# Token-major one-hot tiles for the gate matrices of two PEER stages, all made by VectorE

## The chip, the cores and the metric

One core of a Trainium2 chip runs the whole program. The metric is the device time of one execution in microseconds (us); less is better.

## The reference, cut to what matters

The program is two transformer layers over 512 tokens of width 1024. Each ends in a PEER feed-forward step, which picks 16 of 16384 experts for each of 8 heads and each token:

```python
def peer_ffn(h, w_query, sub_keys, expert_u, expert_v):
    def chunk(xc):                                   # 128 tokens
        q = (xc @ w_query).reshape(128, 8, 2, 128)
        s1 = einsum('thc,hnc->thn', q[:, :, 0], sub_keys[:, 0])
        s2 = einsum('thc,hnc->thn', q[:, :, 1], sub_keys[:, 1])
        ...                                          # top 16 of each, then top 16 of the sums
        eidx = e1 * 128 + e2                         # (t, 8, 16): 128 experts a token
        gate = softmax(top)
        act = gelu(einsum('td,thkd->thk', xc, expert_u[eidx]))
        return einsum('thk,thkd->td', gate * act, expert_v[eidx])
```

## The kernel before, in words

The kernel does a PEER step in three stages.

*Route.* The expert indices (`E`, `ei`) and the gates (`GT`) are found for all 512 tokens; VectorE does the top-16 searches.

*Gate matrices* (lines 1160 to 1213), for the first 384 tokens (`ND = 3` tiles of 128; the fourth tile is done by gathered rows, in the main loop). A token has 128 slots (8 heads by 16), and its gates are wanted as a dense matrix of 128 by 128 over all 16384 experts. An expert's number has 14 bits: 3 high ones, 4 middle ones and 7 low ones. They are transposed so that the slots lie on the partitions and the tokens along the free dimension (`sT[0]`, `sT[1]`, `sT[2]` in bf16; `sT[3]` holds the gates in fp32). For each group of `TG = 32` tokens three small tiles are made: `oa_` (one-hot of the 3 high bits, then times the gate) and `ob_` (one-hot of the 4 middle bits). For each 8 tokens two large ones follow: `oh2` (one-hot of the low 7 bits, 128 columns a token) and `oh1` (the product of `oa_` and `ob_`, again 128 columns a token). One fp32 matmul a token, `oh2` transposed times `oh1`, is the token's matrix. The profile records an fp32 matmul as two instructions, so that 384 tokens make 768 records a stage. Four tokens share a PSUM tile (`pgg`, two buffers); ScalarE copies it into a staging tile `stg`, and two DMAs a group write that to DRAM (`Gd`), 12 groups a stage. In the profile `oha`, `ohb` and `oh` are these tiles.

Both large tiles have the layout (128 columns, 8 tokens), tokens innermost: a token's operand in the matmul, `oh2[:, :, 4 * q + j]`, takes one fp32 element in every eight, 32 bytes apart. Of the `oh1` products VectorE makes one in four and GpSimd three.

*Main loop* (from line 1259): 128 steps over blocks of 128 experts. Step e takes the gates of its block from DRAM (`gbuf`, four blocks a load), multiplies them with the activations `ga` of that block (`w`, VectorE, line 1270), splits the product (`wh` on ScalarE, `wl` on VectorE) and multiplies it with the V rows into `y`. The activations come from a unit A for each block (`emit_A`): a DMA of the U block (`ur`), a rounded copy on ScalarE (`uh`, L1100), the remainder on GpSimd (`ul`, L1106), 24 matmuls into `pa` (L1113, L1114, L1116) and a Gelu on ScalarE. Units run `NA = 28` blocks ahead of the loop: 19 are issued during the routing, `TB = 3` ahead of the gate matrices, 4 among them (`RG`), 2 behind them, so 9 in and around the gate stage.

The routing has a fixed order. In the gate stage each engine's order is made by the scheduler of the framework from the program and its own estimate of costs; each engine then works through its list in order, and waits where an operand or a buffer isn't free.

Of the kernel before, what the change touches and what calls it, by code (L numbers as in the profile page):

```python
# [14 lines left out]
OP = mybir.AluOpType  # L15
# [8 lines left out]
def build(tc, I, out, dbg=None, stop=None):  # L24
# [22 lines left out]
    V, A, G, T, S = nc.vector, nc.scalar, nc.gpsimd, nc.tensor, nc.sync  # L47
# [706 lines left out]
    for h2 in range(2):  # L754
        if h2 == 1:
            ws = keep_w(wk, I["w_mem_o"], 8, 0)
        for t in range(NT):
# [3 lines left out]
            for hh in range(2):  # L761
# [10 lines left out]
                for j in range(2):  # L772
# [3 lines left out]
                            in1=zs.unsqueeze(2).broadcast_to([128, 2, 256]), op=OP.mult)  # L776
# [59 lines left out]
        o_ += 16 // (i + 1)  # L836
    NC = o_ + 8
    CE = G
    O1 = 3
    TA = 3  # L840
    GS = 2
    GE = 99
# [3 lines left out]
    EF = 120  # L846
    EV = 100
    EW = 120
    GM = 4
    GR = 3  # L850
    TB = 3
    NA = 28

    def queries(qp, Wq, hi, lo):
# [197 lines left out]
    TG = 32  # L1052
# [18 lines left out]
    def peer(keysT_d, U, UT, Vt, front, finish, nm, side=None, also=None, then=None):  # L1071
# [37 lines left out]
        def a_mm(e):  # L1109
# [46 lines left out]
        r1 = rp.enter_context(tc.tile_pool(name=nm + "r1", bufs=1))  # L1156
# [3 lines left out]
        iota = r1.tile([128, 128], F32, name="iota")  # L1160
# [8 lines left out]
        sT = [r1.tile([128, NDT], F32 if j == 3 else BF16, name=f"sT{j}") for j in range(4)]  # L1169
# [7 lines left out]
        ix.close()  # L1177
        run_ahead(TB)
        rw = rp.enter_context(tc.tile_pool(name=nm + "gg", bufs=2))
        irep = r1.tile([128, 128, 8], BF16, name="irep")  # L1180
        V.tensor_copy(out=irep, in_=iota.unsqueeze(2).broadcast_to([128, 128, 8]))
        irtg = r1.tile([128, 16, TG], BF16, name="irtg")
        V.tensor_copy(out=irtg, in_=iota[:, 0:16].unsqueeze(2).broadcast_to([128, 16, TG]))
        for tg in range(NTG):
            stg = rw.tile([128, 128, TG], F32, name="stg", tag="stg")

            def row(j, c0, n, m):
                return sT[j][:, c0:c0 + n].unsqueeze(1).broadcast_to([128, m, n])

            c0 = tg * TG  # L1190
            oa_ = rw.tile([128, 8, TG], F32, name="oha", tag="oha")
            V.tensor_tensor(out=oa_, in0=irtg[:, 0:8], in1=row(0, c0, TG, 8), op=OP.is_equal)
            V.tensor_tensor(out=oa_, in0=oa_, in1=row(3, c0, TG, 8), op=OP.mult)
            ob_ = rw.tile([128, 16, TG], F32, name="ohb", tag="ohb")
            V.tensor_tensor(out=ob_, in0=irtg, in1=row(1, c0, TG, 16), op=OP.is_equal)
            for t8 in range(TG // 8):
                tk = slice(t8 * 8, t8 * 8 + 8)
                oh2 = rw.tile([128, 128, 8], F32, name="oh2", tag="oh2")
                V.tensor_tensor(out=oh2, in0=irep, in1=row(2, c0 + t8 * 8, 8, 128), op=OP.is_equal)  # L1199
                oh1 = rw.tile([128, 128, 8], F32, name="oh1", tag="oh1", bufs=O1)  # L1200
                (V if (tg * 4 + t8) % GM == GR else G).tensor_tensor(
                    out=oh1.rearrange("p (a b) t -> p a b t", a=8), in0=oa_[:, :, tk].unsqueeze(2).broadcast_to([128, 8, 16, 8]),
                    in1=ob_[:, :, tk].unsqueeze(1).broadcast_to([128, 8, 16, 8]), op=OP.mult)
                for q in range(2):
                    pg = psm.tile([128, 4, 128], F32, name="pgg", tag="mm")
                    for j in range(4):
                        T.matmul(pg[:, j, :], oh2[:, :, 4 * q + j], oh1[:, :, 4 * q + j], start=True, stop=True)  # L1207
                    ts = t8 * 8 + 4 * q
                    A.copy(out=stg[:, :, ts:ts + 4].rearrange("p e t -> p t e"), in_=pg)
            S.dma_start(out=Gd[0][:, tg], in_=stg[:, 0:G0])  # L1210
            S.dma_start(out=Gd[1][:, tg], in_=stg[:, G0:])
            if tg in RG:
                run_ahead(1)
        vrs = {e: load_v(e) for e in range(2)}
        rp.close()
        pctx.close()
        run_ahead(NA)
        nev = 0
# [40 lines left out]
        for e in range(128):  # L1259
# [9 lines left out]
            with tc.manual_schedule(engines={mybir.EngineType.Pool, DVE_}):  # L1269
# [24 lines left out]
            for t in range(ND):  # L1294
                ts = slice(t * 128, (t + 1) * 128)
# [9 lines left out]
        row = then() if then else (lambda t, psum: None)  # L1305
# [102 lines left out]
    if stop == "h2":  # L1408
# [347 lines left out]
    def fin2(t, acc, pool, psum):  # L1756
# [116 lines left out]
```

## Time and profile before

| | us |
|---|---|
| median of 3 runs | 4033.55 |
| lowest, highest | 4032.31, 4042.46 |
| the profiled execution | 4039.25 |
| its span | 4037.5 |
| start of the first gate stage (first `oha`) to first `y` matmul | 743.04 to 970.62 |
| the same of the second | 2859.16 to 3086.76 |

TensorE is busy for 96% of the span, VectorE for 77%, GpSimd for 53%, ScalarE for 41%. The two gate stages are the stretches from about 743 to 970 us and from 2859 to 3087 us. A share over the span says little of them; they are read from windows, from the groups of instructions by line in that stretch, and from the timeline. In a timeline a row's first two numbers are its start and its length; instructions of one engine overlap a little, so the step from one start to the next is what an instruction costs in a dense row of them.

### The profile page before, as it was taken

How to read it: one execution, taken by the hardware profiler on the slowest of the kernel's cores; microseconds unless marked ns; L12 is line 12 of the kernel's file. 1: busy time of each engine (PE TensorE's matmuls, PEld its weight loads, DVE VectorE, ACT ScalarE, POOL GpSimd, SP SyncE). 2: the span in 40 equal slices, each digit the busy share in tenths (PEclk: the TensorE clock that was granted, in tenths of full speed). 3: DMA queues.
4: the chain of work that ended last, by engine and by line, in shares of the span. 5: the costliest groups of instructions: out<-in, count | busy, mean ns of one | idle time of the engine just before them, and what ended most of it. 6: DMA issues, size and time to landing. Idle time of an engine off the chain costs nothing. (4 is left out here: it accounts for less than half of the span.)

```text
span 4037.5 us, 53263 instructions
## 1 busy us (share of the span) xinstructions
PE 3859.8 (96%) x19062; PEld 3367.6 (83%) x19062; DVE 3101.3 (77%) x5460; ACT 1659.2 (41%) x2567; POOL 2146.8 (53%) x1333
## 2 busy tenths in 40 slices
PE   6999999899999999999899988999899999999999
PEld 5767788899899999987777766788899999999987
DVE  8456589884898888877756566689885898888875
ACT  3454432454333333333444567332454333333333
POOL 3000047654788887750424433257655778887750
PEclk8999999999999999999999989999999999999999
DMA  3333132235999889987222322332236999999884
GB/s 112 98 102 115 61 112 74 103 133 195 313 332 316 314 315 314 328 286 261 91 81 58 93 73 93 116 111 78 106 136 218 320 324 316 315 317 314 303 272 151
DMA packets 330057, 784.31 MB, mean 194 GB/s; under 512 B 32048, under 2 KB 148864, under 8 KB 326400
## 3 DMA queue, kind: packets, MB, share of 16 engines
q1 hardware_dynamic: 252608, 499.86, 37.6%
q0 software_dynamic: 77184, 281.05, 19.5%
q8 instruction: 150, 2.46, 0.2%
q14 instruction: 115, 0.94, 0.1%
HBM read 722.98 MB, written 56.65 MB: 193 GB/s over the span
## 5 line engine op out<-in xcount | busy, mean ns | idle before, releaser
L1106 POOL TENSOR_TENSOR ul<-ur,uh 128x1024 fp32r<-128x1024 f32 x256 | 713.7, 2788 | 263.9 <-ACT uh L1100 177.1
L1113 PE MATMUL pa<-phi,uh 128*128 128x384 f32 x2048 | 695.1, 339 | 0.6 <-ACT ga L1118 0.6
L1114 PE MATMUL pa<-plo,uh 128*128 128x384 f32 x2048 | 694.2, 339 | 0.0
L1300 PE MATMUL y<-vl,wh 128*128 128x512 f32 x1536 | 599.8, 392 | 5.7 <-DVE vl L1273 5.7
L1301 PE MATMUL y<-vh,wl 128*128 128x512 f32 x1536 | 601.8, 393 | 0.0
L1299 PE MATMUL y<-vh,wh 128*128 128x512 f32 x1536 | 595.6, 392 | 1.7 <-ACT vh L1272 1.6
L1273 DVE TENSOR_TENSOR vl<-vr,vh 128x1024 fp32r<-128x1024 f32 x256 | 341.4, 1334 | 216.1 <-ACT vh L1272 215.9
L1248 DVE SCALAR_TENSOR_TENSOR acc<-vrow,act,acc 128x1024 f32<-128x1024 f32 x256 | 423.6, 1655 | 50.0 <-DMA vrow<-in_expert_v_dram,ei 25.3
L1237 DVE SCALAR_TENSOR_TENSOR urow<-urow,hgat 128x1024 f32<-128x1024 f32 x256 | 416.5, 1634 | 28.9 <-DMA urow<-in_peer_u_dram,ei 17.4
L1271 ACT CAST wh<-w 128x384 fp32r<-128x384 f32 x256 | 131.4, 513 | 745.8 <-PE y L1300 607.0
L1116 PE MATMUL pa<-phi,ul 128*128 128x384 f32 x2048 | 403.9, 340 | 18.5 <-POOL ul L1106 18.4
L1100 ACT CAST uh<-ur 128x1024 fp32r<-128x1024 f32 x256 | 269.6, 1053 | 356.6 <-issue 233.4
L1113 PEld LDWEIGHTS pa<-phi,uh 128*128 128x128 f32 x2048 | 388.7, 190 | 9.8 <-ACT ga L1118 1.0
L1114 PEld LDWEIGHTS pa<-plo,uh 128*128 128x128 f32 x2048 | 388.8, 190 | 9.6
L1116 PEld LDWEIGHTS pa<-phi,ul 128*128 128x128 f32 x2048 | 362.9, 190 | 21.0 <-POOL ul L1106 21.0
L1207 PE MATMUL pgg<-oh,oh 128*128 128x128 f32 x1536 | 373.8, 421 | 4.8 <-DVE oh L1199 4.0
L1207 PEld LDWEIGHTS pgg<-oh,oh 128*128 128x128 f32 x1536 | 369.9, 337 | 7.2 <-issue 5.0
L1301 PEld LDWEIGHTS y<-vh,wl 128*128 128x128 f32 x1536 | 288.7, 188 | 65.8 <-DVE wl L1274 2.7
L1300 PEld LDWEIGHTS y<-vl,wh 128*128 128x128 f32 x1536 | 289.0, 188 | 64.6 <-DVE vl L1273 9.5
L1299 PEld LDWEIGHTS y<-vh,wh 128*128 128x128 f32 x1536 | 288.4, 188 | 57.4 <-ACT vh L1272 4.0
L77 DVE TENSOR_TENSOR wl<-wr,wh 128x512 fp32r<-128x512 f32 (+1 forms) x276 | 201.4, 738 | 146.9 <-ACT wh L76 146.8
L1270 DVE TENSOR_TENSOR w<-gbuf,ga 128x384 f32<-128x384 f32 x256 | 261.8, 1024 | 45.7 <-DMA ur<-in_expert_uT_dram 21.6
(538 smaller groups left out, 7662.9 us busy)
## 6 DMA issues: line engine op xcount, KB each, us to landing
vr<-in_peer_v_dram SPq DMA_DIRECT2D x128, 512.0 KB, 6.2
ur<-in_peer_uT_dram SPq DMA_DIRECT2D x128, 512.0 KB, 4.1
vr<-in_expert_v_dram SPq DMA_DIRECT2D x128, 512.0 KB, 6.7
ur<-in_expert_uT_dram SPq DMA_DIRECT2D x128, 512.0 KB, 4.3
gbuf<-Gd SPq DMA_DIRECT2D x64, 768.0 KB, 9.7
Gd<-stg SPq DMA_DIRECT2D x24, 1920.0 KB, 6.1
wr<-in_w_in_dram SPq DMA_DIRECT2D x104, 256.0 KB, 2.7
war<-in_w_ada_dram SPq DMA_DIRECT2D x24, 512.0 KB, 6.9
```

Source lines behind the costliest of these rows:

```text
L1100: A.copy(out=uh, in_=ua[e])
L1106: G.tensor_tensor(out=ul, in0=raw, in1=uh.bitcast(F32), op=OP.subtract)
L1113: T.matmul(pa, uh[:, k, :], hi[:, k, 0:NDT], start=(k == 0), stop=False)
L1114: T.matmul(pa, uh[:, k, :], lo[:, k, 0:NDT], start=False, stop=False)
L1116: T.matmul(pa, ul[:, k, :], hi[:, k, 0:NDT], start=False, stop=(k == 7))
L1207: T.matmul(pg[:, j, :], oh2[:, :, 4 * q + j], oh1[:, :, 4 * q + j], start=True, stop=True)
L1237: V.scalar_tensor_tensor(out=row, in0=row, scalar=1.0, in1=hg_, op0=OP.mult, op1=OP.mult, accum_out=act[:, k:k + 1])
L1248: V.scalar_tensor_tensor(out=acc, in0=rows_.pop((1, k)), scalar=act[:, k:k + 1], in1=acc, op0=OP.mult, op1=OP.add)
L1273: V.tensor_tensor(out=vl, in0=vr, in1=vh.bitcast(F32), op=OP.subtract)
L1299: T.matmul(y[t][c], wh[:, ts], vh[:, cs_], start=(e_ == 0), stop=False)
L1300: T.matmul(y[t][c], wh[:, ts], vl[:, cs_], start=False, stop=False)
L1301: T.matmul(y[t][c], wl[:, ts], vh[:, cs_], start=False, stop=(e_ == 127))
```

## The change

The large tiles get the layout (8 tokens, 128 columns), so that a token's 128 columns lie side by side; the small ones (32 tokens, 8 or 16 columns). The comparison takes the column numbers from one row of 128 (`iob`), repeated for each token, and the token's bits repeated along the columns (step 0 in the innermost dimension). The two index tiles made ahead of the stage (`irep`, `irtg`) go. All products `oh1` are made by VectorE, and `oh1` has two buffers in place of three.

```diff
-        irep = r1.tile([128, 128, 8], BF16, name="irep")
-        V.tensor_copy(out=irep, in_=iota.unsqueeze(2).broadcast_to([128, 128, 8]))
-        irtg = r1.tile([128, 16, TG], BF16, name="irtg")
-        V.tensor_copy(out=irtg, in_=iota[:, 0:16].unsqueeze(2).broadcast_to([128, 16, TG]))
+        iob = r1.tile([128, 128], BF16, name="iob")
+        V.tensor_copy(out=iob, in_=iota)
+        def eq_row(out, n, m, j, c0):
+            V.tensor_tensor(out=out, in0=iob[:, 0:m].unsqueeze(1).broadcast_to([128, n, m]),
+                            in1=sT[j][:, c0:c0 + n].unsqueeze(2).broadcast_to([128, n, m]), op=OP.is_equal)
...
-            for t8 in range(TG // 8):
-                tk = slice(t8 * 8, t8 * 8 + 8)
-                oh2 = rw.tile([128, 128, 8], F32, name="oh2", tag="oh2")
-                V.tensor_tensor(out=oh2, in0=irep, in1=row(2, c0 + t8 * 8, 8, 128), op=OP.is_equal)
-                oh1 = rw.tile([128, 128, 8], F32, name="oh1", tag="oh1", bufs=O1)
-                (V if (tg * 4 + t8) % GM == GR else G).tensor_tensor(
-                    out=oh1.rearrange("p (a b) t -> p a b t", a=8), in0=oa_[:, :, tk].unsqueeze(2).broadcast_to([128, 8, 16, 8]),
-                    in1=ob_[:, :, tk].unsqueeze(1).broadcast_to([128, 8, 16, 8]), op=OP.mult)
+            for tk in range(0, TG, TK):
+                oh2 = rw.tile([128, TK, 128], F32, name="oh2", tag="oh2")
+                eq_row(oh2, TK, 128, 2, c0 + tk)
+                oh1 = rw.tile([128, TK, 128], F32, name="oh1", tag="oh1")
+                V.tensor_tensor(out=oh1.rearrange("p t (a b) -> p t a b", a=8), in0=oa_[:, tk:tk + TK].unsqueeze(3).broadcast_to([128, TK, 8, 16]),
+                                in1=ob_[:, tk:tk + TK].unsqueeze(2).broadcast_to([128, TK, 8, 16]), op=OP.mult)
...
-                        T.matmul(pg[:, j, :], oh2[:, :, 4 * q + j], oh1[:, :, 4 * q + j], start=True, stop=True)
+                        T.matmul(pg[:, j, :], oh2[:, q + j, :], oh1[:, q + j, :], start=True, stop=True)
```

Line numbers in the changed kernel are smaller by two to four: `pa` is L1111, L1112 and L1114 there, `pgg` L1204, `y` L1295 to L1297.

The scheduler orders the engines anew. On TensorE, early in the first gate stage of the kernel before (`pgg` is the gate matmuls, `pa` a unit A):

```order
L1207 MATMUL pgg<-oh_7320,oh_7318 128x128 x8
L1207 MATMUL pgg<-oh_7336,oh_7334 128x128 x8
L1207 MATMUL pgg<-oh_7360,oh_7358 128x128 x8
L1113 MATMUL pa<-phi,uh 128x384
L1114 MATMUL pa<-plo,uh 128x384
L1113 MATMUL pa<-phi,uh 128x384
L1207 MATMUL pgg<-oh_7376,oh_7374 128x128 x8
L1207 MATMUL pgg<-oh_7392,oh_7390 128x128 x8
```

Here 72 tokens of gate matmuls run in one block before the first `pa`. On TensorE in the changed kernel, at the same place:

```order
L1204 MATMUL pgg<-oh_7214,oh_7212 128x128 x8
L1204 MATMUL pgg<-oh_7230,oh_7228 128x128 x8
L1111 MATMUL pa<-phi,uh 128x384
L1112 MATMUL pa<-plo,uh 128x384
L1111 MATMUL pa<-phi,uh 128x384
L1112 MATMUL pa<-plo,uh 128x384
L1204 MATMUL pgg<-oh_7246,oh_7244 128x128 x8
L1111 MATMUL pa<-phi,uh 128x384
L1112 MATMUL pa<-plo,uh 128x384
L1111 MATMUL pa<-phi,uh 128x384
L1204 MATMUL pgg<-oh_7262,oh_7260 128x128 x8
```

From the second 8 tokens on, two to four matmuls of a unit A now stand behind every 8 tokens (nine or ten behind every 32). At the end of the stage, on TensorE in the kernel before, four whole units stand between the last gate matmul and the first `y` (the first and the last rows of these 96 matmuls):

```order
L1207 MATMUL pgg<-oh_8139,oh_8137 128x128 x8
L1207 MATMUL pgg<-oh_8155,oh_8153 128x128 x8
L1113 MATMUL pa<-phi,uh 128x384
L1114 MATMUL pa<-plo,uh 128x384
...
L1116 MATMUL pa<-phi,ul 128x384 x8
L1299 MATMUL y_8282<-vh,wh 128x512
L1300 MATMUL y_8282<-vl,wh 128x512
```

And in the changed kernel, at the same place on TensorE:

```order
L1204 MATMUL pgg<-oh_8121,oh_8119 128x128 x8
L1114 MATMUL pa<-phi,ul 128x384 x2
L1204 MATMUL pgg<-oh_8137,oh_8135 128x128 x8
L1204 MATMUL pgg<-oh_8153,oh_8151 128x128 x8
L1295 MATMUL y_8280<-vh,wh 128x512
L1296 MATMUL y_8280<-vl,wh 128x512
L1297 MATMUL y_8280<-vh,wl 128x512
```

All nine units now end before the last gate matmul; nothing stands between it and the first `y`. On VectorE the rows of one 32-token group in the changed kernel (L1184 is `eq_row`, L1192 the gate times `oa_`, L1199 the product `oh1`):

```order
L1184 TENSOR_TENSOR oha<-iob,sT_7074 128x256
L1184 TENSOR_TENSOR ohb<-iob,sT_7075 128x512
L1192 TENSOR_TENSOR oha<-oha,sT_7077 128x256
L1184 TENSOR_TENSOR oh_7356<-iob,sT_7076 128x1024
L1199 TENSOR_TENSOR oh_7358<-oha,ohb 128x1024
L1184 TENSOR_TENSOR oh_7372<-iob,sT_7076 128x1024
L1199 TENSOR_TENSOR oh_7374<-oha,ohb 128x1024
L1184 TENSOR_TENSOR oh_7388<-iob,sT_7076 128x1024
L1199 TENSOR_TENSOR oh_7390<-oha,ohb 128x1024
L1184 TENSOR_TENSOR oh_7404<-iob,sT_7076 128x1024
L1199 TENSOR_TENSOR oh_7406<-oha,ohb 128x1024
```

It was one such product in a group on VectorE before, and three on GpSimd; now it is four on VectorE.

## Rows read from the trace of the kernel before

**Rows 1.** The page: busy time of each engine over the span.
```profile
PE 3859.8 (96%) x19062; PEld 3367.6 (83%) x19062; DVE 3101.3 (77%) x5460; ACT 1659.2 (41%) x2567; POOL 2146.8 (53%) x1333
```
**Rows 2.** Windows: stretch, its length, busy us of PE, PEld, DVE, ACT, POOL, PEclk, DMA.
```profile
720.00:730.00 10.00, 6.20 (x20) 6.20 (x21) 9.90 (x49) 0.63 (x1) 8.24 (x11) 0.66 0.14 52
...
850.00:900.00 50.00, 49.86 (x215) 49.59 (x214) 40.35 (x24) 25.63 (x26) 28.85 (x10) 1.00 0.34 137
...
2850.00:2855.00 5.00, 0.16 (x1) 0.00 (x0) 5.00 (x7) 1.10 (x3) 3.92 (x2) 0.80 0.35 109
2855.00:2860.00 5.00, 4.73 (x20) 4.54 (x21) 1.64 (x5) 2.85 (x7) 0.00 (x0) 0.52 0.29 104
```
**Rows 3.** Groups by line, 752 to 985 us: count, busy us, mean ns, idle before.
```profile
L1207 PE MATMUL pgg<-oh,oh 128*128 128x128 f32 x768 | 186.9, 421 | 2.8 <-DVE oh L1199 2.4
L1207 PEld LDWEIGHTS pgg<-oh,oh 128*128 128x128 f32 x768 | 184.9, 337 | 4.0 <-issue 3.8
...
L1209 ACT COPY stg<-pgg 128x512 f32<-128x512 f32 x96 | 99.0, 1031 | 93.7 <-PE pgg L1207 93.7
L1199 DVE TENSOR_TENSOR oh<-irep,sT 128x1024 f32<-128x1024 bf16 x46 | 88.5, 1924 | 42.8 <-PE pgg L1207 41.8
```
**Rows 4.** Groups by line, whole span: fp32 matmuls of 128 columns, side by side.
```profile
L910 PE MATMUL psc<-keysT,qs 128*128 128x128 f32 x256 | 33.8, 275 | 1.8 <-ACT qs L900 1.8
...
L910 PEld LDWEIGHTS psc<-keysT,qs 128*128 128x128 f32 x256 | 33.0, 191 | 2.0 <-ACT qs L900 2.0
```
**Rows 5.** Timeline, TensorE: three matmuls of a unit A in a dense row.
```profile
744.50 0.34 PE L1113 MATMUL pa<-phi,uh 128*128 128x384 f32 x1
...
744.68 0.34 PE L1114 MATMUL pa<-plo,uh 128*128 128x384 f32 x1
...
744.85 0.34 PE L1113 MATMUL pa<-phi,uh 128*128 128x384 f32 x1
```
**Rows 6.** Timeline, VectorE: the stage's start, two large tiles, the second stage's start.
```profile
743.04 0.42 DVE L1192 TENSOR_TENSOR oha<-irtg,sT 128x256 f32<-128x256 bf16 x1 [2.91 <-PE ptE L1175]
743.39 0.68 DVE L1195 TENSOR_TENSOR ohb<-irtg,sT 128x512 f32<-128x512 bf16 x1
743.99 0.42 DVE L1192 TENSOR_TENSOR oha<-irtg,sT 128x256 f32<-128x256 bf16 x1
744.33 1.22 DVE L1199 TENSOR_TENSOR oh<-irep,sT 128x1024 f32<-128x1024 bf16 x1
745.46 2.63 DVE L1193 TENSOR_TENSOR oha<-oha,sT 128x256 f32<-128x256 f32 x1
...
942.66 1.23 DVE L1199 TENSOR_TENSOR oh<-irep,sT 128x1024 f32<-128x1024 bf16 x1 [2.61 <-PE pgg L1207]
943.80 1.22 DVE L1201 TENSOR_TENSOR oh<-oha,ohb 128x1024 f32<-128x1024 f32 x1
...
2859.16 0.42 DVE L1192 TENSOR_TENSOR oha<-irtg,sT 128x256 f32<-128x256 bf16 x1 [3.36 <-PE ptE L1175]
```
**Rows 7.** By line: VectorE operations with a step-0 innermost operand (ns min/median/max).
```profile
L1048 DVE TENSOR_TENSOR GT<-GT,zz x2: 673/673/673, 738.9 to 2854.6; 128x512 f32<-128x512 f32 x2
...
L966 DVE TENSOR_TENSOR ec<-eq,cidx x4: 983/988/1606, 725.1 to 2848.4; 128x800 f32<-128x800 bf16 x4
```
**Rows 8.** Timeline, GpSimd: a `ul` beside VectorE's row at 745.46.
```profile
744.80 3.01 POOL L1106 TENSOR_TENSOR ul<-ur,uh 128x1024 fp32r<-128x1024 f32 x1 [6.56 <-PE pa L1116]
```
**Rows 9.** Timeline: last gate matrix to first `y`; last row, second stage's first `y`.
```profile
954.16 1.10 ACT L1209 COPY stg<-pgg 128x512 f32<-128x512 f32 x1 [0.91 <-PE pgg L1207]
962.66 0.55 SPq L1262 DMA_DIRECT2D gbuf<-Gd  x1
...
969.20 0.56 DVE L1270 TENSOR_TENSOR w<-gbuf,ga 128x384 f32<-128x384 f32 x1 [21.48 <-POOL ul L1106]
...
970.62 0.39 PE L1299 MATMUL y<-vh,wh 128*128 128x512 f32 x1
...
3086.76 0.39 PE L1299 MATMUL y<-vh,wh 128*128 128x512 f32 x1
```

More of the change, by code (lines that the diff above doesn't have):

```diff
@@ L838, in build @@
     CE = G
-    O1 = 3
     TA = 3
@@ L848, in build @@
     EW = 120
-    GM = 4
-    GR = 3
     TB = 3
+    TK = 8
     NA = 28
@@ L1184, in peer @@
         for tg in range(NTG):
             stg = rw.tile([128, 128, TG], F32, name="stg", tag="stg")
-            def row(j, c0, n, m):
-                return sT[j][:, c0:c0 + n].unsqueeze(1).broadcast_to([128, m, n])
             c0 = tg * TG
[L1191 to L1194, printed above, removed]
@@ L1195, in peer @@
-            V.tensor_tensor(out=ob_, in0=irtg, in1=row(1, c0, TG, 16), op=OP.is_equal)
-            for t8 in range(TG // 8):
-                tk = slice(t8 * 8, t8 * 8 + 8)
-                oh2 = rw.tile([128, 128, 8], F32, name="oh2", tag="oh2")
-                V.tensor_tensor(out=oh2, in0=irep, in1=row(2, c0 + t8 * 8, 8, 128), op=OP.is_equal)
-                oh1 = rw.tile([128, 128, 8], F32, name="oh1", tag="oh1", bufs=O1)
-                (V if (tg * 4 + t8) % GM == GR else G).tensor_tensor(
-                    out=oh1.rearrange("p (a b) t -> p a b t", a=8), in0=oa_[:, :, tk].unsqueeze(2).broadcast_to([128, 8, 16, 8]),
-                    in1=ob_[:, :, tk].unsqueeze(1).broadcast_to([128, 8, 16, 8]), op=OP.mult)
-                for q in range(2):
+            oa_ = rw.tile([128, TG, 8], F32, name="oha", tag="oha")
@@ new lines, in peer @@
+            eq_row(oa_, TG, 8, 0, c0)
+            V.tensor_tensor(out=oa_, in0=oa_, in1=sT[3][:, c0:c0 + TG].unsqueeze(2).broadcast_to([128, TG, 8]), op=OP.mult)
+            ob_ = rw.tile([128, TG, 16], F32, name="ohb", tag="ohb")
+            eq_row(ob_, TG, 16, 1, c0)
+            for tk in range(0, TG, TK):
[4 more added lines that the diff above has]
+                                in1=ob_[:, tk:tk + TK].unsqueeze(2).broadcast_to([128, TK, 8, 16]), op=OP.mult)
+                for q in range(0, TK, 4):
@@ L1205, in peer @@
                     pg = psm.tile([128, 4, 128], F32, name="pgg", tag="mm")
                     for j in range(4):
-                        T.matmul(pg[:, j, :], oh2[:, :, 4 * q + j], oh1[:, :, 4 * q + j], start=True, stop=True)
-                    ts = t8 * 8 + 4 * q
-                    A.copy(out=stg[:, :, ts:ts + 4].rearrange("p e t -> p t e"), in_=pg)
+                        T.matmul(pg[:, j, :], oh2[:, q + j, :], oh1[:, q + j, :], start=True, stop=True)
+                    A.copy(out=stg[:, :, tk + q:tk + q + 4].rearrange("p e t -> p t e"), in_=pg)
```

## The prediction

> **What bounds the kernel now.** I read the busy shares first: TensorE works for 96% of the span [rows 1], so a gain has to come from TensorE's work, or from a stretch where it waits. The change touches two stretches alone, the gate stages: from the first `oha` to the first `y` they last 970.62 - 743.04 = 227.6 us and 3086.76 - 2859.16 = 227.6 us [rows 6, 9]. Then the windows: in the middle of a stage TensorE is busy for 49.86 of 50 us at the full clock, VectorE for 40.35, ScalarE for 25.63 and GpSimd for 28.85 [rows 2]. The groups by line agree: the gate matmuls waited 2.8 us in all, while ScalarE waited 93.7 us and VectorE 41.8 us for them [rows 3]. TensorE bounds the stage.
>
> What holds TensorE there? 768 records fill 186.9 us, 0.243 us each, or 0.487 us a token; a weight load takes 337 ns and a matmul 421 ns from start to end [rows 3]. The routing's scores are the same operation, fp32 128x128 by 128x128, with both operands side by side in memory: 256 records in 33.8 us, 0.132 us each, 191 ns and 275 ns [rows 4]. Between the two groups only the reading of the operands differs, 32 bytes from element to element against 4.
>
> **TensorE after the change.** With operands side by side I take the price of rows 4: 768 x 0.132 = 101.4 us, so 85.5 us less of TensorE work a stage. Of the nine units A, seven (168 matmuls) now lie between the first and the last gate matmul; a matmul starts every 0.173 us [rows 5], 29.1 us. From the first gate matmul TensorE thus needs 130.5 us. That matmul comes some 8 us after the first `oha` (the small tiles, three large ones and one or two delays by GpSimd, all priced below).
>
> **VectorE after the change.** It makes 96 large tiles a stage. Two in a row start 943.80 - 942.66 = 1.14 us apart [rows 6]: 109.4 us. Each of the 12 groups has three small operations, at steps of 0.35, 0.60 and 0.34 us in the rows at 743 us [rows 6] (the multiplication, of the first one's shape, at the last): 1.29 x 12 = 15.5 us. The large comparison now repeats one operand with step 0 innermost. Two operations of before do so: 512 elements in 673 ns and 800 in 983 ns [rows 7], against 680 ns for 512 without it [rows 6]. I cost the layout at nothing on VectorE.
>
> GpSimd's products end, but its `ul` of the nine units stay. While a `ul` runs, VectorE stands: the `oha` product at 745.46 took 2.63 us where an operation of that shape takes 0.42, beside a `ul` from 744.80 to 747.81 [rows 6, 8]. I charge 2.2 us for each of nine, 19.9 us. The sum for VectorE is 109.4 + 15.5 + 19.9 = 144.8 us.
>
> TensorE, at 8 + 130.5 = 138.5 us, ends before VectorE, at 144.8 + 2.1 (its last 8 tokens). So VectorE becomes the bound, by 8 us only. That is close enough for the two to hinder each other. `oh1` and `oh2` have two buffers each, and both engines work in order: behind every 32 tokens stand nine or ten matmuls of a unit, 1.7 us, while VectorE makes small tiles for 1.29 us; the excess, 0.4 us, delays the next group's buffers. Twelve of these make 5 us; I take 6 us for all stalls and keep 0 to 29 us (below) as bounds. ScalarE's copies, 99.0 us [rows 3], and its nine `uh` and Gelus stay under both.
>
> **The end of the stage.** From the end of the last copy, 955.26, to the first `y`, 970.62, a chain of DMAs runs: the last group to DRAM, `gbuf` back (issued at 962.66), then `w` at 969.20 [rows 9]. Its 15.4 us were covered: 96 matmuls of units A stood there, 96 x 0.173 = 16.6 us of work that had to be done anyway. In the new order they stand inside the stage, and nothing covers the chain. The work isn't lost, but TensorE waits for 15.4 us. [...]
>
> **The sum.** A stage takes 144.8 + 6 + 2.1 (last 8 tokens) + 1.1 (last copy) + 15.4 + 2 = 171.4 us in place of 227.6: 56.2 us less. The main loop behind it is left as it was, in order and in work, so I carry all of it to the end. The two index tiles that go were made during the routing; I count their about 1 us as nothing. Two stages: 112 us. The profiled execution took 4039.25 us, so 3927 us; the median is 5.7 us lower, and I predict **3921 us** in its terms. The likeliest case's own range is 3900 to 3945.
>
> **Rivals.**
>
> *TensorE stays the bound (lower).* If a `ul` costs VectorE little, being fitted into its waits, VectorE needs 124.9 us and TensorE's 138.5 rule: 138.5 + 1.1 + 15.4 = 155.0, a gain of 72.6 us a stage: 3888 us. For it: the two are close. Against: VectorE has no waits then.
>
> *The units A don't overlap (higher).* A unit's matmuls are strewn among the gate matmuls and wait for `ur`, `uh` and `ul`, whose DMA stands in SyncE's queue behind writes of `Gd` that wait for ScalarE. With two buffers VectorE can run only 16 tokens ahead. If all seven units were to cost their full time beside VectorE's, 29.1 us more a stage: 3979 us.
>
> *The layout isn't what costs.* If a token's matmul keeps its 0.243 us a record, TensorE needs 8 + 186.9 + 29.1 + 1.1 + 15.4 + 2 = 242.5 us a stage, since the tail is bare now: 4063 us. Against it stand rows 4.
>
> *VectorE is slowed by the step-0 operand (slower).* Its place is the 96 large tiles. Apart from these a stage takes 171.4 - 109.4 = 62.0 us, so it decides from (227.6 - 62.0) / 96 = 1.73 us a tile, half as much again as 1.14. At twice the time, 2.28 us, a stage takes 280.9 us: 4140 us. Rows 7 speak against it.
> [...]
>
> [...]
> [...]
>
> **How the numbers follow.** Forecast 0.60, TensorE as the bound 0.13, units not overlapped 0.15, layout without effect 0.04, step-0 operand 0.03, clock 0.03, and 0.02 for losses that just eat the gain. About 0.3%, 12 us, is what a measurement of this kernel can tell from no change. The first three are faster, 0.88; the three before the last are slower, 0.10; the last is the same, 0.02. The range reaches to the first two rivals, 3885 to 3982: it leaves out the 0.12 of the last four and a little of the first three.
>
> **What would show it.** Right: `pgg` records near 275 ns and weight loads near 191; 768 of them in some 101 us if merged; VectorE busy for over nine tenths of the stage with large tiles 1.14 us apart and about 3.4 us beside a `ul`; TensorE idle for some 15 us ahead of the first `y`, ended by `w`; first `oha` to first `y` near 171 us. Wrong: `pgg` still at 421 ns, large tiles alone over 1.7 us, a granted clock under 0.8 through the stage, or a main loop that is longer than before.

## The result and the profile after

| us | before | after |
|---|---|---|
| median of 4 runs (lowest to highest) | 4032.93 (4029.94 to 4042.46) | 3911.80 (3903.53 to 3913.65) |
| the profiled execution, its span | 4039.25, 4037.5 | 3913.65, 3911.9 |
| first gate stage, first `oha` to first `y` | 227.6 | 742.89 to 909.95: 167.1 |
| second gate stage | 227.6 | 2794.97 to 2965.27: 170.3 |
| first `y` to the second stage's first `oha` | 1888.5 | 1885.0 |
| second stage's first `y` to the end of the span | 950.7 | 946.6 |

The ratio is 0.9692 [0.967, 0.9713]: faster by 121 us. Of the 125.6 us between the two profiled executions, the gate stages hold 60.5 + 57.3 = 117.8 us and the two main loops (with the second routing) 3.5 + 4.1 = 7.6 us.

The page's row of busy times answers to [rows 1]. Its first number is each engine's busy time:

```profile
PE 3677.0 (94%) x19062; PEld 3173.3 (81%) x19062; DVE 3065.2 (78%) x5530; ACT 1649.7 (42%) x2567; POOL 1957.0 (50%) x1261
```

TensorE has the same 19062 records and 182.8 us less of busy time: the records are shorter, not fewer. Windows of the first stage, with the columns of [rows 2] (busy us of PE, PEld, DVE, ACT, POOL, then the granted clock):

```profile
743.00:893.00 150.00, 133.76 (x1004) 126.72 (x1004) 148.34 (x132) 107.16 (x115) 40.57 (x11) 1.00 0.50 191
800.00:850.00 50.00, 44.67 (x344) 42.12 (x342) 49.48 (x47) 36.55 (x40) 12.69 (x3) 1.00 0.55 215
893.00:910.00 17.00, 1.58 (x15) 1.39 (x13) 1.21 (x2) 4.51 (x6) 4.11 (x5) 0.64 0.71 239
910.00:915.00 5.00, 5.00 (x12) 3.68 (x13) 3.97 (x7) 2.69 (x5) 0.00 (x0) 0.51 1.05 390
```

In the middle of the stage TensorE was busy for 49.86 of 50 us and VectorE for 40.35; now it is 44.67 and 49.48. The bound has changed hands, and in this stage the granted clock stays at 1.00, although TensorE waits. Then come 17 us in which no engine is busy for long, and 5 us with TensorE at a granted clock of 0.51. The groups by line of the first stage, 742 to 910 us, answer to [rows 3]:

```profile
L1204 PE MATMUL pgg<-oh,oh 128*128 128x128 f32 x768 | 96.4, 279 | 16.2 <-DVE oh L1199 15.5 <-ACT stg L1205 0.5
L1205 ACT COPY stg<-pgg 128x512 f32<-128x512 f32 x96 | 96.4, 1100 | 37.2 <-PE pgg L1204 32.2 <-issue 3.5 <-ACT ga L1116 1.4
L1204 PEld LDWEIGHTS pgg<-oh,oh 128*128 128x128 f32 x768 | 90.4, 191 | 23.3 <-issue 13.5 <-ACT stg L1205 8.0
L1184 DVE TENSOR_TENSOR oh<-iob,sT 128x1024 f32<-128x1024 bf16 x48 | 68.1, 1420 | 1.0 <-PE pgg L1204 0.8
L1199 DVE TENSOR_TENSOR oh<-oha,ohb 128x1024 f32<-128x1024 f32 x48 | 66.9, 1396 | 0.0
L1104 POOL TENSOR_TENSOR ul<-ur,uh 128x1024 fp32r<-128x1024 f32 x11 | 40.6, 3688 | 113.1 <-PE pa L1114 68.6 <-ACT stg L1205 42.9 <-ACT uh L1098 1.6
L1111 PE MATMUL pa<-phi,uh 128*128 128x384 f32 x80 | 28.2, 353 | 0.0
```

Read the idle columns as a pair. Before, `oh` waited 41.8 us for `pgg`; now `pgg` waits 15.5 us for `oh` (nine waits of 1.05 to 2.37 us in TensorE's timeline, each behind a tile that a `ul` made late), and `oh` waits 0.8 us. The 768 records take 96.4 us in place of 186.9, 0.126 us each, with 279 ns a matmul and 191 ns a load, as in the scores [rows 4]. `ul` counts eleven, and `pa` has 80 records of L1111 where eight make a unit: ten units. The same view of before, 742 to 971 us, has nine:

```profile
L1113 PE MATMUL pa<-phi,uh 128*128 128x384 f32 x72 | 25.0, 347 | 0.0
```

VectorE's timeline, the columns of [rows 6] (start, length):

```profile
742.89 0.43 DVE L1184 TENSOR_TENSOR oha<-iob,sT 128x256 f32<-128x256 bf16 x1 [3.36 <-PE ptE L1173]
...
786.53 1.21 DVE L1184 TENSOR_TENSOR oh<-iob,sT 128x1024 f32<-128x1024 bf16 x1
787.66 1.21 DVE L1199 TENSOR_TENSOR oh<-oha,ohb 128x1024 f32<-128x1024 f32 x1
788.87 1.23 DVE L1184 TENSOR_TENSOR oh<-iob,sT 128x1024 f32<-128x1024 bf16 x1
790.01 3.40 DVE L1199 TENSOR_TENSOR oh<-oha,ohb 128x1024 f32<-128x1024 f32 x1
793.34 1.21 DVE L1184 TENSOR_TENSOR oh<-iob,sT 128x1024 f32<-128x1024 bf16 x1
...
888.98 3.38 DVE L1199 TENSOR_TENSOR oh<-oha,ohb 128x1024 f32<-128x1024 f32 x1
```

Two tiles in a row start 1.13 to 1.21 us apart; the one at 790.01 takes 3.40 us, since GpSimd runs this beside it (its timeline):

```profile
789.50 2.83 POOL L1104 TENSOR_TENSOR ul<-ur,uh 128x1024 fp32r<-128x1024 f32 x1 [10.93 <-PE pa L1114]
```

The end of the stage, from the timeline (SPq is SyncE's queue), answers to [rows 9]:

```profile
893.67 1.91 ACT L1205 COPY stg<-pgg 128x512 f32<-128x512 f32 x2 [2.45 <-PE pgg L1204]
895.61 0.32 SPq L1206 DMA_DIRECT2D Gd<-stg  x1
895.97 0.43 SPq L1207 DMA_DIRECT2D Gd<-stg  x1
902.88 1.30 SPq L1258 DMA_DIRECT2D gbuf<-Gd  x2
908.79 0.56 DVE L1266 TENSOR_TENSOR w<-gbuf,ga 128x384 f32<-128x384 f32 x1 [16.43 <-DMA gbuf<-Gd]
909.95 0.80 PE L1295 MATMUL y<-vh,wh 128*128 128x512 f32 x1 [15.42 <-ACT wh L1267]
...
2965.27 0.79 PE L1295 MATMUL y<-vh,wh 128*128 128x512 f32 x1 [14.89 <-ACT wh L1267]
```

From the last copy's end, 895.58, it takes 14.4 us to the first `y`; TensorE stands for 15.4 us with nothing to do. The first `y` takes 0.80 us where it took 0.39.

So the first stage adds up: VectorE from 742.89 to 892.36 (888.98 + 3.38), 149.5 us; the last tile's matmuls and copies 3.2 us; the chain 14.4 us; 167.1 us in all.

### The profile page after: what moved, and what is told of

The parts are those of the page before. It is cut to its first block, busy times and chain, and to the rows that moved or that the text cites. A ratio compares the mean times of both kernels' runs of the same rounds, so it can differ in the third digit from the quotient of the medians.

```text
span 3911.9 us, 53171 instructions
## 1 busy us (share of the span) xinstructions
PE 3677.0 (94%) x19062; PEld 3173.3 (81%) x19062; DVE 3065.2 (78%) x5530; ACT 1649.7 (42%) x2567; POOL 1957.0 (50%) x1261
## 5 line engine op out<-in xcount | busy, mean ns | idle before, releaser
L1104 POOL TENSOR_TENSOR ul<-ur,uh 128x1024 fp32r<-128x1024 f32 x256 | 739.3, 2888 | 424.9 <-ACT uh L1098 195.5
L1111 PE MATMUL pa<-phi,uh 128*128 128x384 f32 x2048 | 696.4, 340 | 1.5 <-ACT ga L1116 1.5
L1112 PE MATMUL pa<-plo,uh 128*128 128x384 f32 x2048 | 695.7, 340 | 0.0
L1295 PE MATMUL y<-vh,wh 128*128 128x512 f32 x1536 | 597.0, 393 | 32.7 <-ACT wh L1267 30.3
L1297 PE MATMUL y<-vh,wl 128*128 128x512 f32 x1536 | 602.1, 393 | 0.0
L1269 DVE TENSOR_TENSOR vl<-vr,vh 128x1024 fp32r<-128x1024 f32 x256 | 350.4, 1369 | 225.0 <-ACT vh L1268 177.5
L1114 PE MATMUL pa<-phi,ul 128*128 128x384 f32 x2048 | 409.5, 341 | 15.3 <-POOL ul L1104 15.2
L1111 PEld LDWEIGHTS pa<-phi,uh 128*128 128x128 f32 x2048 | 388.9, 190 | 10.7 <-ACT ga L1116 1.9
L1112 PEld LDWEIGHTS pa<-plo,uh 128*128 128x128 f32 x2048 | 388.7, 190 | 9.5
L1114 PEld LDWEIGHTS pa<-phi,ul 128*128 128x128 f32 x2048 | 361.1, 190 | 17.5 <-POOL ul L1104 17.5
L1295 PEld LDWEIGHTS y<-vh,wh 128*128 128x128 f32 x1536 | 289.0, 189 | 89.1 <-ACT wh L1267 30.8
L1297 PEld LDWEIGHTS y<-vh,wl 128*128 128x128 f32 x1536 | 289.3, 189 | 65.4 <-DVE wl L1270 2.0
L1268 ACT CAST vh<-vr 128x1024 fp32r<-128x1024 f32 x256 | 267.6, 1046 | 44.4 <-DMA vr<-in_peer_v_dram 29.5
L76 ACT CAST wh<-wr 128x512 fp32r<-128x512 f32 (+1 forms) x276 | 149.2, 551 | 205.2 <-PE mm L120 124.6
```

Of the source, the lines that this page charges most:

```text
L1104: G.tensor_tensor(out=ul, in0=raw, in1=uh.bitcast(F32), op=OP.subtract)
L1111: T.matmul(pa, uh[:, k, :], hi[:, k, 0:NDT], start=(k == 0), stop=False)
L1112: T.matmul(pa, uh[:, k, :], lo[:, k, 0:NDT], start=False, stop=False)
L1268: A.copy(out=vh, in_=vr)
L1269: V.tensor_tensor(out=vl, in0=vr, in1=vh.bitcast(F32), op=OP.subtract)
L1295: T.matmul(y[t][c], wh[:, ts], vh[:, cs_], start=(e_ == 0), stop=False)
```

## Experiments

The theory: the layout shortens TensorE's records from 0.243 to about 0.13 us, VectorE thereby becomes the bound, and the bare DMA chain at the end gives a part of the gain back. The rivals: the gain comes from the engine that makes the products; TensorE is the bound still; one operand alone is what costs. Ratios are each to the kernel before, timed beside it. The lengths of the two stages in each trace stand in a table behind E10.

### E1: the engine alone

The kernel before, with all products on VectorE and two buffers.

```diff
-                oh1 = rw.tile([128, 128, 8], F32, name="oh1", tag="oh1", bufs=O1)
-                (V if (tg * 4 + t8) % GM == GR else G).tensor_tensor(
+                oh1 = rw.tile([128, 128, 8], F32, name="oh1", tag="oh1")
+                V.tensor_tensor(
```

> The tiles keep the layout of before (tokens innermost); all products are made by VectorE, with two buffers. TensorE's order is that of the changed kernel, row by row. Theory (the strided reading of the operands is what is removed): the gate records keep 0.243 us each, TensorE bounds the stage and the DMA chain at its end is bare: 8 + 186.9 + 33.2 (eight units A, one of them out of the main loop) + 1.1 + 15.4 + 2 = 246.6 us a stage, 4.15 of it taken from the main loop; that is 15 us a stage more than before, about 4063 us. Rival (the engine and the order make the gain): about 3912 us, as the changed kernel.

Measured: 4061.05 us (4055.1 to 4070.51), 1.0079 [1.0053, 1.0105]. Slower than before by 29 us. The window in mid-stage:

```profile
800.00:850.00 50.00, 50.00 (x221) 49.70 (x221) 32.05 (x28) 24.68 (x26) 6.01 (x2) 1.00 0.38 145
```

TensorE has no gap, with 221 records where the changed kernel has 344; VectorE has room. Its stages last 246.3 and 246.5 us, as expected. The new order and the engine without the layout only bare the chain, at the price that the rival "the layout isn't what costs" gave (4063).

### E2: the layout alone

The changed kernel, with the products shared as before and three buffers.

```diff
-                oh1 = rw.tile([128, TK, 128], F32, name="oh1", tag="oh1")
-                V.tensor_tensor(out=...
+                oh1 = rw.tile([128, TK, 128], F32, name="oh1", tag="oh1", bufs=3)
+                (V if (tg * 4 + tk // 8) % 4 == 3 else G).tensor_tensor(out=...
```

> The tiles have the layout of the changed kernel; GpSimd makes three of four products with three buffers, and TensorE's order is that of before. Theory (VectorE and GpSimd take turns): VectorE's 60 large tiles 68.4 + small ones 15.5 + 36 products and 9 to 11 remainders of GpSimd at 2.2 us each = 183 to 188 us, then 3.2 and the DMA chain, covered by units A, 15.4: some 205 us a stage, 45 us less for both than before, about 3988 us; the gate records at 275 ns. Rival (the layout alone makes the gain and who makes the products is of no account): TensorE's sum of 8 + 101.4 + 33.2 rules, some 148 us a stage, about 3875 us.

Measured: 3940.69 us (3931.08 to 3944.08), 0.9763 [0.9736, 0.979]; my figure was 47 us too high. I had let each operation of GpSimd hold VectorE up by the 2.2 us of before. The timelines' records by tile (ns min/median/max), first of the kernel before, then of E2:

```profile
L1201 POOL TENSOR_TENSOR oh<-oha,ohb x72: 2370/3325/3430, 748.2 to 3055.0; 128x1024 f32<-128x1024 f32 x72
```

```profile
L1199 POOL TENSOR_TENSOR oh<-oha,ohb x72: 2102/2902/2926, 747.0 to 2967.7; 128x1024 f32<-128x1024 f32 x72
```

The same product is shorter by 423 ns at the median in E2. 36 of them a stage make 15.2 us, two stages 30 us; if all of it is on the path, that is 30 of the 47. Summed over the timeline of E2's first stage, VectorE's tiles are 73 us longer than undisturbed, for 45 operations of GpSimd: 1.6 us each, where I had charged 2.2. So the layout alone gives 92 us; making all tiles on VectorE adds 29 us on top of it, though in the old layout it cost 29 us (E1). The second part of the change is worth something only behind the first. E2's groups by line, 741 to 924 us, show the short records, and what the second part spares:

```profile
L1204 PE MATMUL pgg<-oh,oh 128*128 128x128 f32 x768 | 103.4, 291 | 40.5 <-DVE oh L1184 34.3 <-issue 3.2 <-ACT stg L1205 2.8
...
L1184 DVE TENSOR_TENSOR oh<-iob,sT 128x1024 f32<-128x1024 bf16 x48 | 83.5, 1754 | 6.6 <-PE pgg L1204 6.6
...
L1184 DVE TENSOR_TENSOR oha<-iob,sT 128x256 f32<-128x256 bf16 x12 | 22.3, 1862 | 3.0 <-PE ptE L1173 3.0
```

The records take 103.4 us with the products still made by GpSimd. A comparison takes 1754 ns in the mean here and 1420 in the changed kernel, the small `oha` 1862 ns against some 420 when undisturbed. The products on GpSimd make VectorE stand too, as a `ul` does.

### E3 and E4: one operand each

E3 gives only the weights (`oh2`) the new layout, E4 only the moving operand (`oh1`); products are on VectorE in both. The matmul's line, of E3 against the kernel before, of E4 against the changed one:

```diff
# E3
-                        T.matmul(pg[:, j, :], oh2[:, :, 4 * q + j], oh1[:, :, 4 * q + j], start=True, stop=True)
+                        T.matmul(pg[:, j, :], oh2[:, 4 * q + j, :], oh1[:, :, 4 * q + j], start=True, stop=True)
# E4
-                        T.matmul(pg[:, j, :], oh2[:, q + j, :], oh1[:, q + j, :], start=True, stop=True)
+                        T.matmul(pg[:, j, :], oh2[:, :, q + j], oh1[:, q + j, :], start=True, stop=True)
```

> Of the two matmul operands only oh2, which is loaded as weights, is token-major; oh1, which is streamed, keeps tokens innermost. All on VectorE, order as in the changed kernel. If the two reads follow one another on TensorE, each strided one costs half of the difference, (0.243 - 0.132) / 2 = 0.056 us a record: 0.188 us, a stage of 8 + 144.4 + 33.2 + 18.5 = 204 us, about 3984 us. If they run beside one another, the streamed one still rules at 0.243 us: about 4063 us, as with the old layout. If only the weight load matters: about 3912 us.

> The reverse: only oh1, which is streamed, is token-major; oh2, the weights, keeps tokens innermost. All on VectorE, order as in the changed kernel. If the two reads follow one another: 0.188 us a record, about 3984 us, the same as with the weights alone. If they run beside one another: the weight load rules at 0.243 us, about 4063 us. If only the streamed operand matters: about 3912 us.

Measured: E3 4048.87 us (ten runs, 4035.51 to 4059.74), 1.0037 [1.0021, 1.0052]; E4 4050.4 us (ten runs, 4037.66 to 4061.79), 1.0039 [1.0021, 1.0056]. Records by tile (ns min/median/max), E3 first:

```profile
L1208 PEld LDWEIGHTS pgg<-oh,oh x1536: 186/208/313, 755.5 to 3096.1; 128*128 128x128 f32 x192
L1208 PE MATMUL pgg<-oh,oh x1536: 390/412/447, 755.7 to 3096.3; 128*128 128x128 f32 x192
```

```profile
L1206 PEld LDWEIGHTS pgg<-oh,oh x1536: 312/335/340, 752.5 to 3078.0; 128*128 128x128 f32 x192
L1206 PE MATMUL pgg<-oh,oh x1536: 328/402/504, 752.6 to 3078.2; 128*128 128x128 f32 x192
```

And their groups by line in the first stage, E3 (745 to 985 us) first:

```profile
L1208 PE MATMUL pgg<-oh,oh 128*128 128x128 f32 x768 | 186.9, 411 | 0.8 <-DVE oh L1202 0.6
```

```profile
L1206 PE MATMUL pgg<-oh,oh 128*128 128x128 f32 x768 | 188.2, 399 | 0.8 <-DVE oh L1201 0.6
```

In E3 the load falls to 208 ns and the matmul keeps 412; in E4 the load keeps 335 ns and the matmul 402. The pace is 0.243 and 0.245 us a record, not the 0.188 of reads that follow one another. Either way some 11 to 12 us of E1's 4061 go, of the 149 us that both together bring (4061 to 3912); none of the three times expected was met, but 4063 is by far the nearest. In the 50 us from 800 us the loads are busy for 45.26 us (E3) and 49.63 us (E4), the matmuls for 49.91 and 49.92: the two run beside one another, and one that takes an element in every 32 bytes is enough to hold the pair near the old pace.

### E5: more work for VectorE

The first `oh2` of each group is made twice: 12 large tiles more a stage, 13.7 us.

```diff
                 eq_row(oh2, TK, 128, 2, c0 + tk)
+                if tk == 0:
+                    eq_row(oh2, TK, 128, 2, c0 + tk)
```

> The changed kernel with one large comparison in every 32 tokens made twice: 12 more VectorE operations a stage, 13.7 us. Theory (VectorE now bounds the stage): 13.7 us a stage more, about 3939 us. Rival (TensorE still bounds it, VectorE has 8 us or more to spare): at most 6 us a stage, 3912 to 3924 us.

Measured: 3939.89 us (3935.74 to 3950.45), 0.9772 [0.975, 0.9794]. 28 us for the 27.4 us added: all of it is on the path. That the two agree so well is partly luck: in the trace the stages are 19.4 and 15.1 us longer, not 13.7. In the first, VectorE waited 4.8 us for `pgg`, 4 us more than in the changed kernel, with a granted clock of 0.97 from 800 to 850 us, where the changed kernel has 1.00.

### E6: more work for TensorE

One matmul in eight is done twice: 48 fp32 matmuls more a stage, 12.7 us.

```diff
                         T.matmul(pg[:, j, :], oh2[:, q + j, :], oh1[:, q + j, :], start=True, stop=True)
+                    if q == 0:
+                        T.matmul(pg[:, 3, :], oh2[:, 3, :], oh1[:, 3, :], start=True, stop=True)
```

> The changed kernel with one gate matmul in every 8 tokens made twice: 48 more fp32 matmuls a stage, 12.7 us on TensorE. The scheduler then leaves 56 matmuls of units A behind the last gate matmul, under the DMA chain. Theory (VectorE bounds the stage; TensorE waited for some 16 us in it and 15 behind it): no change, 3907 to 3917 us. Rival (TensorE bounds it): 12.7 us a stage more, about 3937 us.

Measured: 3907.35 us (3895.91 to 3909.8), 0.969 [0.9671, 0.971], the changed kernel's time within the noise. Its window:

```profile
800.00:850.00 50.00, 45.91 (x359) 43.07 (x360) 48.76 (x47) 36.35 (x40) 5.84 (x3) 1.00 0.54 214
```

VectorE makes as many tiles (47) as in the changed kernel's window. Alone this run is a weak test: as expected, 56 matmuls of `pa` (9.7 us) stand behind the last gate matmul, no longer among them, so that TensorE's list there grew by 3 us a stage and not by 12.7. What settles the bound is E5 and the waits in the changed kernel, 15.5 us of TensorE for VectorE and 0.8 us the other way: it is VectorE.

### E7: `ul` on VectorE

The remainders of the units run ahead go from GpSimd to VectorE, so that GpSimd doesn't hold VectorE up.

```diff
-        def a_lo(e):
+        def a_lo(e, g=G):
...
-            G.tensor_tensor(out=ul, in0=raw, in1=uh.bitcast(F32), op=OP.subtract)
+            g.tensor_tensor(out=ul, in0=raw, in1=uh.bitcast(F32), op=OP.subtract)
...
-                emit_A(e)
+                emit_A(e, V)
```

> The changed kernel with the remainders ul of the nine units A issued around the gate stage made by VectorE in place of GpSimd. Theory (a ul on GpSimd makes VectorE stand for 2.2 us, on VectorE it costs 1.14): 9.5 us a stage less on VectorE, 4 us of it given back since the scheduler leaves the tenth unit in the main loop: 3896 to 3903 us. Rival (a ul on GpSimd costs VectorE next to nothing): 10 us a stage more, about 3932 us.

Measured: 3882.73 us (3868.55 to 3885.73), 0.9621 [0.9597, 0.9645]: 29 us under the changed kernel, more than expected (3896 to 3903). The window that holds VectorE's whole dense stretch (from the first `oha`, 739.57), then its timeline at the end, then the large tiles' groups by line (739 to 891 us):

```profile
739.57:869.57 130.00, 118.23 (x904) 111.25 (x902) 129.19 (x135) 99.89 (x105) 0.00 (x0) 1.00 0.49 196
```

```profile
868.66 1.22 DVE L1199 TENSOR_TENSOR oh<-oha,ohb 128x1024 f32<-128x1024 f32 x1
869.80 2.35 DVE L1104 TENSOR_TENSOR ul<-ur,uh 128x1024 fp32r<-128x1024 f32 x2
...
886.84 0.89 DVE L1266 TENSOR_TENSOR w<-gbuf,ga 128x384 f32<-128x384 f32 x1 [8.63 <-DMA gbuf<-Gd]
```

```profile
L1184 DVE TENSOR_TENSOR oh<-iob,sT 128x1024 f32<-128x1024 bf16 x48 | 58.7, 1223 | 0.8 <-PE pgg L1204 0.5
L1199 DVE TENSOR_TENSOR oh<-oha,ohb 128x1024 f32<-128x1024 f32 x48 | 58.5, 1219 | 0.0
```

The last large tile ends 130.3 us after the first `oha`, in place of 149.5. GpSimd is idle throughout that stretch, and no tile is lengthened any more: 1223 and 1219 ns in the mean, for 1420 and 1396. TensorE's list is lighter too, with 106 matmuls of `pa` among the gate matmuls and 64 behind them, but VectorE is busy for 129.19 of the 130 us and waits 0.5 us for `pgg`: it is the bound here as well. What I had missed: only three `ul` fall into that stretch (two at 746.66, one at 847.68); the scheduler puts most of the last three units' work into the chain's time, where TensorE and VectorE have nothing else to do.

### E8 and E9: the chain at the end

E8 gives `gbuf` memory of its own, so that its load needn't wait until the stage's memory is free; `stg` gets its own pool too, and two pools of the main loop change places. E9 also has SyncE issue the first load ahead of the last, larger write.

```diff
+        gbp = px.enter_context(tc.tile_pool(name=nm + "gb", bufs=2, side="right"))
...
-                gbuf = tb_.tile([128, NTG, EB, TG], F32, name="gbuf", tag="gbuf")
+                gbuf = gbp.tile([128, NTG, EB, TG], F32, name="gbuf", tag="gbuf")
# E9 also, in the last group
-            S.dma_start(out=Gd[1][:, tg], in_=stg[:, G0:])
+                    S.dma_start(out=gb0, in_=Gd[0][:, :, 0:EB, :])
+                    S.dma_start(out=Gd[1][:, tg], in_=stg[:, G0:])
```

> The changed kernel with other places in memory alone: gbuf in a pool of its own, the main loop's w, vh, vl buffers where the one-hot tiles were and not where stg was; TensorE's order is unchanged. Theory (at the end of a stage gbuf waits for its buffer, until the last large write out of stg has ended): gbuf starts when the small write of its own data has landed, some 4 to 8 us earlier a stage: 3896 to 3904 us. Rival (the transfers themselves fill the 15 us): no change, about 3912 us.

> The kernel with early buffers, and in the last group of a stage SyncE issues the first load of gbuf ahead of the large write out of stg instead of behind it. Theory (in the run before, the load of gbuf took 9 us since it shared the DMA engines with the large write): the load lands within some 4 us of its issue, the first y starts about 5 us earlier a stage: 3893 to 3900 us. Rival (the read of the small write's data is what takes long): no change against early buffers, 3903 to 3909 us.

Measured: E8 3905.6 us (3903.16 to 3909.12), 0.9687 [0.9668, 0.9707]; E9 3895.29 us (3890.33 to 3904.5), 0.9651 [0.963, 0.9671]. Timelines, E8 first:

```profile
896.39 0.43 SPq L1209 DMA_DIRECT2D Gd<-stg  x1
897.84 2.26 SPq L1260 DMA_DIRECT2D gbuf<-Gd  x2
906.84 0.56 DVE L1268 TENSOR_TENSOR w<-gbuf,ga 128x384 f32<-128x384 f32 x1 [14.06 <-DMA gbuf<-Gd]
```

```profile
896.10 0.55 SPq L1212 DMA_DIRECT2D gbuf<-Gd  x1
896.71 0.86 SPq L1213 DMA_DIRECT2D Gd<-stg  x1
902.40 0.56 DVE L1275 TENSOR_TENSOR w<-gbuf,ga 128x384 f32<-128x384 f32 x1 [11.62 <-DMA gbuf<-Gd]
```

In E8 the load is issued 1.5 us behind the large write, in the changed kernel 6.9 (895.97 to 902.88), but `w` starts only 2.4 us sooner behind that write: right behind it a load takes 9.0 us to `w`, not the 5.9 of 902.88 to 908.79. Issued ahead of the write (E9) it takes 6.3. So the chain held two costs, the wait for memory and the company of the write. From the last copy's end to the first `y` it lasts 14.4 and 13.9 us in the changed kernel's two stages, 12.0 and 11.9 in E8, 9.6 and 9.6 in E9.

By the whole time E8's gain can't be told from none: its interval and the changed kernel's overlap, and 3905.6 lies between what theory and rival gave. E9 is some 16 us under the changed kernel; the chain holds 9 us of that.

### E10: E7, E8 and E9 together

> Remainders on VectorE around the gate stage, early buffers and the first gbuf load ahead of the large write, together. If the chain at the end of the stage still bounds there, 3 to 6 us a stage less than with the remainders on VectorE alone (3883 us): 3871 to 3877 us. If the 64 matmuls of units A behind the last gate matmul, and their uh and ul, bound there instead: no change, 3880 to 3886 us.

Measured: 3864.76 us (3860.72 to 3875.57), 0.9574 [0.9552, 0.9595]. It beats both kernels: some 48 us under the changed one by the ratios, (0.9692 - 0.9574) x 4033. The gains of E7 (29) and E9 (16) about add up. The time is below the 3871 to 3877 expected, though the stages are shorter than E7's by what was expected, 3.6 and 4.6 us; the rest lies outside them. TensorE's timeline between the last gate matmul and `y`:

```profile
877.81 0.44 PE L1111 MATMUL pa<-phi,uh 128*128 128x384 f32 x1 [2.25 <-ACT uh L1098]
...
887.83 0.40 PE L1304 MATMUL y<-vh,wh 128*128 128x512 f32 x1
```

The longest wait is 2.25 us, for a `uh`, and the first `y` takes 0.40 us, as against 0.39 in the kernel before and 0.80 in the changed one.

**The stages of all runs.** From the first `oha` to the first `y`, in us, read from each trace; beside it what both stages together, and the median time, differ by from the changed kernel:

| run | first | second | both stages | median |
|---|---|---|---|---|
| before | 227.6 | 227.6 | +117.8 | +121.1 |
| changed | 167.1 | 170.3 | | |
| E1 | 246.3 | 246.5 | +155.5 | +149.3 |
| E2 | 182.2 | 181.5 | +26.4 | +28.9 |
| E3 | 239.3 | 240.6 | +142.5 | +137.1 |
| E4 | 240.6 | 241.2 | +144.5 | +138.6 |
| E5 | 186.5 | 185.4 | +34.5 | +28.1 |
| E6 | 168.1 | 166.7 | -2.5 | -4.5 |
| E7 | 151.1 | 151.9 | -34.4 | -29.1 |
| E8 | 166.3 | 167.2 | -3.9 | -6.2 |
| E9 | 163.8 | 162.4 | -11.2 | -16.5 |
| E10 | 147.5 | 147.3 | -42.6 | -47.0 |

The stages tell the runs apart better than the times do: the first main loop with the second routing behind it, which no edit touches but for the tenth unit below, lasts from 1869 to 1889 us in these traces.

## Why the prediction was right, and where its sizes were off

The forecast of 3921 us stands against 3911.8. The first-named case came about: VectorE is the bound, the layout is what pays, the chain lies bare.

**TensorE's record.** 0.132 us was taken from the scores, 0.126 measured, and E1 to E4 show that nothing but the layout of both operands does it. Its rival of 4063 is about E1's time, 4061.

**VectorE's tiles.** The repeated operand was costed at nothing. Large tiles start 1.13 to 1.21 us apart, far from the 1.73 us from which the rival decided, and near the 1.14 us of two in a row before: the repeated element cost nothing that shows here.

**The `ul`.** The step "2.2 us for each of nine, 19.9 us" was too small by the count, not by the price: eleven run in the stage, 24.2 us. With the other terms as forecast, 109.4 + 15.5 + 24.2 = 149.1 us, and VectorE took 149.5. E7 takes the eleven away and adds three of 1.14 us, -20.8 us by this price; it measured -19.2. A large tile beside a `ul` took 3.40 us (790.01), one without 1.21 (787.66); what in the chip makes VectorE stand, no run shows.

**The stalls.** 6 us were charged; VectorE waited 0.8 us for `pgg` in the first stage. My 0.4 us a group did not come about, since the `ul` delays gave TensorE time to catch up: that is argued from the numbers, not tried (in E7 VectorE waits 0.5 us without these delays, but with fewer `pa` in TensorE's list). In the second stage (groups by line, 2794 to 2949 us) the comparison waited longer, which accounts for about 3 of its 3.2 us more:

```profile
L1184 DVE TENSOR_TENSOR oh<-iob,sT 128x1024 f32<-128x1024 bf16 x48 | 70.4, 1466 | 3.9 <-PE pgg L1204 3.8
```

Behind it lies the granted clock. TensorE's timeline there, and a window behind its row (the granted clock is 0.50):

```profile
2845.80 2.79 PE L1204 MATMUL pgg<-oh,oh 128*128 128x128 f32 x16 [1.98 <-DVE oh L1199]
```

```profile
2847.00:2850.00 3.00, 3.00 (x15) 3.00 (x15) 3.00 (x5) 2.07 (x2) 0.00 (x0) 0.50 0.14 55
```

After a wait of 1.98 us, and again after one of 2.04 us (2897.97), TensorE worked some 3 us at a granted clock of 0.50 (2847 to 2850) and 0.51 (2897.97 to 2900.97), and right behind each VectorE waited some 1.5 us for `pgg` (0.31 + 1.17 and 0.29 + 1.17). So a lower clock among the gate matmuls, which has 0.03 among the chances, was at work, at some 3 us in the second stage; why waits as long passed at 1.00 in the first stage is open.

**The end.** The chain: 15.4 forecast, 14.4 and 13.9 measured. The last 2 us in the sum of a stage were charged for a lower clock behind the chain: an estimate, and no run shows that figure. What the runs showed in its place is a granted clock of 0.51 in the 5 us from 910 us and of 0.55 in those from 2965.27 us, where the kernel before has 1.00 in the 5 us from its first `y`: 5 x 0.49 and 5 x 0.45, about 2.5 and 2.3 us lost, as an estimate. This lies behind the first `y`, so the 171.4 us compare as 169.4 with 167.1 and 170.3.

**The main loop.** "Left as it was, in order and in work" was the step that failed, with a small price. I counted nine units A in and around a stage, as before, and seven of them among the gate matmuls. The scheduler had moved a tenth into the stage (80 records of L1111, not 72), with 192 matmuls of `pa` between the first and the last gate matmul, not 168; "All nine units now end before the last gate matmul", in the section on the change, should say ten. TensorE had room for it, 133.76 of 150 us, so by the waits it cost the stage nothing, and each main loop is rid of 24 x 0.173 = 4.15 us. Windows of the second main loop, TensorE's records of `pa` alone, before and after:

```profile
3086.76:4038.00 951.24, 428.82 (x2377) 1.00 0.85 293
```

```profile
2965.27:3912.00 946.73, 424.32 (x2352) 1.00 0.85 292
```

Measured are 3.5 and 4.1 us, of which the lower clock should by the forecast have taken 2. The 3.5 can't be read, since that stretch varies by 20 us from trace to trace. The second loop lasts 948.7 to 950.7 us in the four kernels with nine units (before, E2, E7, E10) and 946.1 to 947.5 us in the eight with ten: some 2.6 us apart, about what 4.15 less the forecast's 2 leaves.

So the two errors on the stage, +4.3 us of `ul` and -5 us of stalls, nearly cancelled, which is luck. In terms of the profiled executions the forecast was 3927 us and 3913.65 were measured, 13 us less: 1.4 us in the stages (116.4 forecast up to the first `y`, 117.8 measured), and 11.6 in the main loops, which I had 4 us longer by the clock and which were 7.6 shorter. Of these 11.6 the tenth unit explains twice 4.15 at most; the rest is within what traces of one kernel differ by. A forecast from the stage's rows alone could have seen the tenth: the order of instructions shows the count of `pa`, and I counted units from the program's text.

One sum was not like the others: the rival with TensorE as the bound leaves out the 2 us of lower clock, and with them gives 3892 us, not 3888.

**What was not told apart.** Why an element every 32 bytes costs what it does; only 32 and 4 bytes were run, and no step between them.

## What to carry to other kernels

Price a matmul by a record of the same shape in the same trace whose operands are laid out as the new ones are, and change both operands: with one left, 11 to 12 of 149 us were gained here (E3, E4). When an engine is freed, work out who is second, how much of the second's time is delay by a third, and what the freed engine was covering: here the second was VectorE, a sixth of its stretch was GpSimd's doing, and the cover lost was a DMA chain of 14 us. Then remove these in turn, as E7 and E9 do; here what each gains about adds up (E10). And compare the stretch that an edit touches, not the whole time alone: outside the stages these traces differ by up to 20 us.

## What the runs showed of the hardware

- One strided operand cost nearly as much as two: loads of 208 ns beside matmuls of 412 (E3), loads of 335 beside matmuls of 402 (E4); only with both side by side are they 191 and 279 (changed kernel), and 0.126 us a record in place of 0.243 to 0.245.
- GpSimd's product of 1024 columns was shorter with the token-major layout, 2902 ns for 3325 at the median, 2102 for 2370 at the least (E2 and the kernel before).
- The load of `gbuf` from DRAM, issued right behind a larger write, took 9.0 us to its user, ahead of it 6.3 (E8, E9).
- Behind TensorE's wait of 15.4 us the granted clock was 0.51 over 5 us (910 to 915 us, changed kernel). In the first stage, with TensorE busy for 133.76 of 150 us and nine waits of 1.05 to 2.37 us, it was 1.00; in the second, waits of 1.98 and 2.04 us were each followed by some 3 us at 0.50 and 0.51.
